# A two-layer hybrid decoder step: the input projection computed in another order of column blocks, and the gating norm's gain and shift moved behind its product

## The chip, the cores and the metric

One Trainium2 chip, one core, one launch. The metric is device time in microseconds (us). In the text PE is the matrix engine, DVE the vector engine, ACT the scalar engine, POOL the GpSimd engine and SP the engine whose queue issues almost all DMAs.

## What is computed

The program runs two layers (DEPTH = 2) over 512 prompt tokens and 32 sample tokens (8 sequences of 4). Each layer mixes tokens in four parallel ways and then runs a feed-forward block. The mixing part of the reference, cut to what matters:

```python
h = rms_norm(x, p['g_mix_pre'])
z = h @ p['w_in']                                   # 1024 -> 2048, fp32
a, ga, u, vb, q, k, v, xd = jnp.split(z, IN_SPLITS, axis=-1)   # 8 blocks of 256 columns
ya = silu(layer_norm(causal_depthwise_conv31(a * sigmoid(ga))))
# gating: LN(v) * g + b, then a causal 128x128 mix per head, plus bias, times gelu(u)
v = layer_norm(gelu(vb), p['sgu_ln_g'], p['sgu_ln_b'])
mixed = einsum('gts,bnsgc->bntgc', tril(w_s), v) + b_s
yb = gelu(u) * mixed
yc = rms_norm(diff_attend(q, k, v_att, lam), attn_sub_g)       # two softmax maps per head
yd = pool_mix(xd)                                   # windows 2, 4, 8, 16
x = x + rms_norm(concat([ya, yb, yc, yd]) @ p['w_out'], g_mix_post)
```

## The kernel before

Every fp32 weight is split into a high part (`whi`, a cast on ACT, line 190) and a low part (`wlo`, a subtraction on DVE, line 193), and a dense product takes three matmuls per 128 rows: high by high, high by low, low by high. The activations (`xhi`, `xlo`) are split in the same way.

`mixing` (one call per layer) walks over the eight 256-column blocks of `w_in` in the order of its table `order`, here by first column: 0 (`a`), 256 (`ga`), 1280 (keys), 1024 (queries), 1536 (values), 1792 (pooling), 512 and 768 (gating). Each block has two steps of 128 columns; each step has a first half (256 tokens) and, two steps later (`LAG = 2`), a second half (256 tokens and the 32 samples). Beside the steps run Python generators that emit the four mixers piece by piece: after each half step `advance` takes the next piece of every active one.

- `taps(c)` and `conv`: the gate product (line 410), then 30 chained multiply-adds of 512 columns on DVE per channel half (line 416), then LayerNorm and the swish. They can start when blocks 0 and 256 are complete.
- `stack`: keys and queries are split and copied by DMA into a 96-row layout. Per channel half that is one output DMA (line 468) and 24 small DMAs on the SP queue (line 478), which has the weight loads too.
- `attention`: per half 8 units of two score matmuls; DVE adds the bias `pb` and takes the minimum (line 501), ACT does the exponential (line 503), DVE forms the weighted difference (lines 511 to 513), PE transposes it (line 516), ACT copies it (line 518), PE multiplies with the values (`oT`).
- `gating`: per 128-token chunk a LayerNorm (lines 339, 340, 595), then a product with the gain and a sum with the shift (lines 596, 597), the causal mix on PE, the bias (line 607), the product (line 610) and a split.
- `pooling`: shifted sums on DVE (line 632).

The output projection (`project_last`, line 1259 onward) needs the split results `ya`, `yb`, `yc`, `yd` of all four. It runs eight turns of 24 matmuls; the first two use the first half of the output columns. In the order of the program the pieces are only a priority: a scheduler puts each engine's instructions in one fixed sequence when the program is built, and each engine then runs its own strictly in that sequence, waiting where one is not ready. The raw blocks of `w_in` have two buffers, the tiles named `t512` (key and query parts, gate) four, the score banks `s` two.

Of the kernel before, what the change touches and what calls it, by code (L numbers as in the profile page):

```python
# [8 lines left out]
F32 = mybir.dt.float32  # L9
# [111 lines left out]
def trunk(ctx, tc, A, O):  # L121
# [154 lines left out]
    def params(l, tp, bank):  # L276
        lam_init = 0.8 - 0.6 * math.exp(-0.3 * l)
        rows = tp.tile([72, 128], F32, tag="prow", name="prow")
        for i, n in enumerate(("conv_b", "conv_ln_g", "conv_ln_b", "pool_scale")):
            SY.dma_start(rows[2 * i:2 * i + 2, :], A[n][l].rearrange("(c p) -> c p", p=128))  # L280
        SY.dma_start(rows[8:70, :], A["conv_w"][l].rearrange("t (c p) -> (t c) p", p=128))
        for i in range(2):
            SY.dma_start(rows[70:71, 64 * i:64 * i + 64], A["attn_sub_g"][l:l + 1, :])
        o = psx(bank)
        T.transpose(o[:, :71], rows[:71, :], ident[:71, :71])
        pf, lm = PF[l][0], PL[l]
        V.tensor_copy(pf[:, :71], o[:, :71])
        V.tensor_scalar(pf[:, 72:76], pf[:, 2:6], 0.5, None, op0=ALU.mult)
        V.tensor_scalar(pf[:, 76:77], pf[:, 70:71], 1.0 - lam_init, None, op0=ALU.mult)
        lq = tp.tile([128, 4, 32], F32, tag="lq", name="lq")  # L290
        for i, n in enumerate(("lambda_q1", "lambda_q2", "lambda_k1", "lambda_k2")):
            SY.dma_start(lq[:, i, :], A[n][l, :].partition_broadcast(128))
        V.tensor_tensor(lq[:, 0:2, :], lq[:, 0:2, :], lq[:, 2:4, :], op=ALU.mult)
        V.tensor_reduce(lm[:, 0:2], lq[:, 0:2, :], axis=AX, op=ALU.add)
        S.activation(lm[:, 0:2], lm[:, 0:2], AF.Exp)
        V.tensor_tensor(lm[:, 2:3], lm[:, 1:2], lm[:, 0:1], op=ALU.subtract)
        V.tensor_scalar(lm[:, 3:4], lm[:, 2:3], -lam_init, None, op0=ALU.add)
# [50 lines left out]
    def mixing(l, mp, early):  # L348
# [32 lines left out]
        def ev_tmp(d, c, f, tag):  # L381
# [13 lines left out]
        order = [  # L395
            (0, [(0, ev_copy(hext[0], 0, 0.5, 30)), (1, ev_copy(hext[1], 1, 0.5, 30))]),
            (256, [(2, ev_ga(0)), (3, ev_ga(1))]),
            (1280, [(10, ev_tmp(kT, 0, 10, "kT")), (11, ev_tmp(kT, 1, 11, "kT"))]),
            (1024, [(8, ev_tmp(qT, 0, 8, "qT")), (9, ev_tmp(qT, 1, 9, "qT"))]),
            (1536, "v"),  # L400
            (1792, [(14, ev_copy(dext[0], 14, 1.0, 15)), (15, ev_copy(dext[1], 15, 1.0, 15))]),
            (512, [(4, ev_copy(uv[:, 0], 4)), (5, ev_copy(uv[:, 1], 5))]),
            (768, [(6, ev_copy(uv[:, 2], 6)), (7, ev_copy(uv[:, 3], 7))]),
        ]

# [52 lines left out]

        def stack():
            for c in range(2):  # L460
                st = ST[c] = {}
# [20 lines left out]
        def attention():  # L482
# [3 lines left out]
            for c in range(2):  # L486
# [20 lines left out]
                def weights(i, hh):  # L507
                    W = 128 * (i + 1)
                    P = Pm.pop((i, hh))
                    dn = den[:, i, hh]  # L510
                    V.reciprocal(dn[:, 2:3], dn[:, 1:2])
                    V.tensor_scalar(dn[:, 3:4], dn[:, 0:1], dn[:, 2:3], nlam, op0=ALU.mult, op1=ALU.mult)
                    V.scalar_tensor_tensor(P[0][:, :W], P[1][:, :W], dn[:, 3:4], P[0][:, :W], op0=ALU.mult, op1=ALU.add)
# [50 lines left out]
        def gating():  # L564
# [3 lines left out]
            for h in range(4):  # L568
                SY.dma_start(bsg[64 * (h % 2):64 * (h % 2) + 64, h // 2, :], A["sgu_b"][l, h, :].partition_broadcast(64))
            gr = mp.tile([128, 2, 256], F32, tag="sgr", name="sgr")  # L570
            SY.dma_start(gr[:, 0, :], A["sgu_ln_g"][l, :].partition_broadcast(128))
            SY.dma_start(gr[:, 1, :], A["sgu_ln_b"][l, :].partition_broadcast(128))
            o = acc()
# [8 lines left out]
            V.tensor_copy(bc, bsg[:, :, 0:4])  # L582
            SG[l] = (wc, bc)
            yield
            for f in (2, 0):
# [4 lines left out]
            for t in range(4):  # L590
# [4 lines left out]
                V.tensor_scalar(vn[:, t, :], o[:, :256], mean, r, op0=ALU.subtract, op1=ALU.mult)  # L595
                V.tensor_tensor(vn[:, t, :], vn[:, t, :], gr[:, 0, :], op=ALU.mult)
                V.tensor_tensor(vn[:, t, :], vn[:, t, :], gr[:, 1, :], op=ALU.add)
                yield
            y = yp.tile([128, 2, 2, SEQ], F32R, tag="y", name="yb")
            for c in range(2):  # L600
                o = acc()
                for n in range(4):
                    for hh in range(2):
                        h = 2 * c + hh
                        mm(o[64 * hh:64 * hh + 64, 128 * n:128 * n + 128], vn[:, n, 64 * h:64 * h + 64], wt[:, h, :])
                t = uv[:, 2 + c, :].rearrange("p (n t) -> p n t", n=4)
                V.tensor_tensor(t, o.rearrange("p (n t) -> p n t", n=4),
                                bsg[:, c:c + 1, :].to_broadcast([128, 4, 128]), op=ALU.add)
                tf = uv[:, 2 + c, :]
# [74 lines left out]
        def load(c0):  # L684
# [4 lines left out]
            else:  # L689
                pairs[c0] = raw_cols(w, c0, V, early.get(c0), None, G if c0 == 0 and early else None)  # L690

# [20 lines left out]
        for u in range(n + LAG):  # L712
# [17 lines left out]
            if b >= 0:  # L730
# [12 lines left out]
                if c0 == 256 and i == 1:  # L743
                    convs.append(taps(1))
                if c0 == 1024 and i == 1:
                    active.append(stack())
                if i == "v":
# [636 lines left out]
    with tc.tile_pool(name="pro", bufs=1, reuse_waits="tile") as pro, \  # L1384
# [6 lines left out]
        g = grow(pro, "g_mix_pre", 0)  # L1391
        early = {0: raw_load(A["w_in"][0], 0)}
        for t in range(2, 5):
            SY.dma_start(xs[t][:rows_of(t)], x_at(0)(128 * t, rows_of(t)))
        early[256] = raw_load(A["w_in"][0], 256)
        for t in range(5):
# [64 lines left out]
```

## Time and profile before

| | |
|---|---|
| median of 3 runs | 1454.04 us (1452.48 to 1457.04) |
| the profiled execution | 1448.71 us |
| its span, first to last instruction | 1446.8 us |
| PE busy / DVE / ACT / POOL | 1372.0 / 823.8 / 504.7 / 262.7 us |
| mean granted clock of PE | 0.978 of full |

The rest of the profiled execution (1.9 us) lies around the span. A busy share is an average over stages; the two mixing stages are about 14 to 192 us and 736 to 907 us of the span, and the feed-forward stages fill most of what is left.

### The profile page before, as it was taken

The numbers are of one execution on the slowest core, as the hardware profiler recorded it, in microseconds if no ns is written. First come the engines' busy times: TensorE is split into PE (matmuls) and PEld (weight loads), VectorE is DVE, ScalarE is ACT, GpSimd is POOL, SyncE is SP. The second block draws the span as 40 slices with busy tenths as digits, with TensorE's granted clock in tenths as the row PEclk, the third lists the DMA queues.
The fourth block names the chain that finished last, engine by engine and source line by source line (L and its number), as shares of the span: only waits on it lengthen the run. The fifth ranks groups of instructions, "written<-read, shape, count | busy, mean of one in ns | idle before, by whom it ended". The sixth has DMA issues, their size and how long they took to land.

```text
span 1446.8 us, 22864 instructions
## 1 busy us (share of the span) xinstructions
PE 1372.0 (95%) x9114; PEld 1078.7 (75%) x9114; DVE 823.8 (57%) x1660; ACT 504.7 (35%) x985; POOL 262.7 (18%) x271
## 2 busy tenths in 40 slices
PE   6999787999999999999989988989999999999997
PEld 6987576877666777777689976777776677768775
DVE  4986759866434333333669976778663333333344
ACT  4346634322224321222343474543322332222231
POOL 1000145455300000000220011544442000000003
PEclk9999799999999999999999997999999999999999
DMA  6452134888848752132434521468877496213132
GB/s 206 116 156 73 59 121 145 301 307 297 296 164 254 241 171 77 59 117 106 150 120 119 146 68 58 163 237 281 318 276 266 153 315 220 81 61 114 59 135 91
DMA packets 160091, 242.15 MB, mean 167 GB/s; under 512 B 10444, under 2 KB 118226, under 8 KB 159986
## 3 DMA queue, kind: packets, MB, share of 16 engines
q1 hardware_dynamic: 141410, 173.32, 37.1%
q0 software_dynamic: 18432, 67.12, 12.4%
q8 instruction: 72, 1.18, 0.3%
q14 instruction: 33, 0.27, 0.1%
q10 hardware_dynamic: 144, 0.26, 0.0%
HBM read 222.33 MB, written 12.04 MB: 162 GB/s over the span
## 4 chain that ended last, share of the span: by engine, by line
PE 81%; DVE 11%; ACT 2%; DMA 2%; issue 2%; POOL 1%; SPq 1%; DVEq 0%; POOLq 0%; ACTq 0%
PE acc L126 61%; PE sx L126 12%; PE ps L126 3%; DVE sca L872 2%; PE s L126 1%; DVE cacc L416 1%; DVE p L501 1%; DVE wlo L193 1%; DVE m L1301 1%; PE oT L126 1%; DVE x_t L1294 1%; ACT whi L190 1%; PE ps L516 1%; SPq L478 1%; PE ps L1001 1%
## 5 line engine op out<-in xcount | busy, mean ns | idle before, releaser
L126 PE MATMUL acc<-xhi,whi 128*128 128x512 f32 (+2 forms) x1152 | 405.5, 353 | 3.2 <-ACT whi L190 2.0
L126 PE MATMUL acc<-xhi,wlo 128*128 128x512 f32 (+2 forms) x1152 | 403.4, 351 | 0.2 <-DVE wlo L193 0.2
L126 PE MATMUL acc<-xlo,whi 128*128 128x512 f32 (+2 forms) x1152 | 402.0, 349 | 1.3 <-DVE xlo L238 1.3
L190 ACT CAST whi<-raw 128x1024 fp32r<-128x1024 f32 x178 | 184.3, 1048 | 333.7 <-PE acc L126 292.8
L193 DVE TENSOR_TENSOR wlo<-raw,whi 128x1024 fp32r<-128x1024 f32 x172 | 217.1, 1268 | 128.7 <-ACT whi L190 126.8
L126 PEld LDWEIGHTS acc<-xhi,whi 128*128 128x128 f32 x1152 | 217.1, 189 | 42.2 <-issue 8.0
L126 PEld LDWEIGHTS acc<-xlo,whi 128*128 128x128 f32 x1152 | 217.2, 189 | 31.9 <-issue 4.1
L126 PEld LDWEIGHTS acc<-xhi,wlo 128*128 128x128 f32 x1152 | 216.9, 188 | 31.5 <-issue 4.7
L126 PE MATMUL acc<-whi,h 128*128 128x512 f32 x704 | 226.7, 397 | 0.0
L126 PEld LDWEIGHTS acc<-whi,h 128*128 128x128 f32 x704 | 131.2, 188 | 44.1 <-issue 11.1
L126 PE MATMUL acc<-wlo,h 128*128 128x512 f32 x352 | 138.6, 395 | 0.0
L1276 POOL TENSOR_TENSOR m<-m,g_g_ffn_post 128x512 f32<-128x512 f32 x14 | 20.1, 1437 | 504.9 <-ACT junk L1275 504.9
L989 DVE STREAM_TRANSPOSE kt<-kr 128x1024 f32<-128x1024 f32 x64 | 78.5, 1233 | 27.6 <-DMA kr<-in_cache_k_dram,ik 23.3
L986 POOL DMA_INDIRECT kr<-in_cache_k_dram,ik x64 | 73.8, 1154 | 100.1 <-DVE kt L989 72.2
L416 DVE SCALAR_TENSOR_TENSOR cacc<-hext,pf,cacc 128x512 f32<-128x512 f32 x120 | 85.4, 747 | 0.6
L1345 DVE SCALAR_TENSOR_TENSOR th<-th,acc 128x512 f32<-128x512 f32 (+1 forms) x46 | 29.9, 649 | 87.2 <-PE acc L126 87.0
L126 PEld LDWEIGHTS acc<-wlo,h 128*128 128x128 f32 x352 | 66.1, 188 | 17.6 <-issue 4.5
L174 POOL TENSOR_TENSOR rsw<-rsw,mhalf 128x1 f32<-128x1 f32 (+2 forms) x62 | 39.1, 636 | 202.9 <-DVE rsw L173 189.4
L1016 POOL DMA_INDIRECT vr<-in_cache_v_dram,iv x64 | 63.2, 988 | 57.0 <-PE sx L126 41.2
L1154 DVE SCALAR_TENSOR_TENSOR sth<-sth,ps 128x64 f32<-128x64 f32 x22 | 4.8, 220 | 86.5 <-ACT sth L1153 86.5
L550 POOL TENSOR_TENSOR rse<-e,mhalf 128x8 f32<-128x8 f32 x4 | 8.5, 2130 | 242.7 <-DVE e L548 242.7
L126 PE MATMUL sx<-vr,pt 128*32 128x256 f32 x512 | 49.3, 381 | 0.0
(401 smaller groups left out, 1864.8 us busy)
## 6 DMA issues: line engine op xcount, KB each, us to landing
raw<-in_w_gu_dram SPq DMA_DIRECT2D x44, 1024.0 KB
raw<-in_w_down_dram SPq DMA_DIRECT2D x20, 1024.0 KB
rws<-in_w_gu_dram SPq DMA_DIRECT2D x40, 512.0 KB
raw<-in_w_in_dram SPq DMA_DIRECT2D x16, 1024.0 KB
raw<-in_w_out_dram SPq DMA_DIRECT2D x8, 1024.0 KB
rwo<-in_w_out_dram SPq DMA_DIRECT2D x16, 512.0 KB
rws<-in_w_down_dram SPq DMA_DIRECT2D x16, 512.0 KB
x<-x_t SPq DMA_DIRECT2D x12, 512.0 KB
```

The source lines that it names most:

```text
L126: T.matmul(out, lhsT, rhs, start=start, stop=stop)
L174: G.tensor_tensor(y, v, mhalf[:P, :n], op=ALU.pow)
L190: S.copy(hi, src)
L193: eng.tensor_tensor(lo, src, hi.bitcast(F32), op=ALU.subtract)
L416: V.scalar_tensor_tensor(a, hext[c][:, t:t + SEQ], pf[:, 8 + 2 * t + c:9 + 2 * t + c], a, op0=ALU.mult, op1=ALU.add)
L478: SY.dma_start(s[32 * g:32 * g + 32, jj, :].bitcast(F32), (hi, lo)[seqs[g]][32 * jj:32 * jj + 32, :].bitcast(F32))
L872: V.scalar_tensor_tensor(a[:, c], ext[:, c, :, t:t + 4], pf[:, 8 + 2 * t + c:9 + 2 * t + c], a[:, c], op0=ALU.mult, op1=ALU.add)
L986: G.indirect_dma_start(out=kr, out_offset=None, in_=ck, in_offset=bass.IndirectOffsetOnAxis(ap=ik[:, s, bg:bg + 1], axis=0))
L989: V.transpose(kt, kr)
L1016: G.indirect_dma_start(out=v.rearrange("p t e -> p (t e)"), out_offset=None, in_=cv, in_offset=bass.IndirectOffsetOnAxis(ap=iv[:, s, a:a + ...
L1276: (V if (t, half) == (3, 1) else G).tensor_tensor(m[t][:, hs], m[t][:, hs], gain[:, hs], op=ALU.mult)
L1345: V.scalar_tensor_tensor(th[:, :n], th[:, :n], 0.5, ou[:, :n], op0=ALU.mult, op1=ALU.mult)
```

## The change

The table `order` becomes keys, queries, values, `a`, `ga`, `u`, `vb`, pooling. `stack` takes the channel half as an argument and starts for each half as soon as its queries are complete. In gating, the gain is applied behind the causal mix (a per-partition factor, read from a parameter tile), and the shift goes through the same mix once per layer and is added to the bias. In attention the two reciprocals of a pair of heads become one instruction on two columns, and so do the two factors. The weights loaded ahead of the first layer are now blocks 1280 and 1024.

```diff
@@ params
+        SY.dma_start(rows[71:73, :], A["sgu_ln_g"][l].rearrange("(c p) -> c p", p=128))
-        T.transpose(o[:, :71], rows[:71, :], ident[:71, :71])
+        T.transpose(o[:, :73], rows[:73, :], ident[:73, :73])
+        V.tensor_copy(pf[:, 77:79], o[:, 71:73])
@@ mixing: order
-            (0, [(0, ev_copy(hext[0], 0, 0.5, 30)), (1, ev_copy(hext[1], 1, 0.5, 30))]),
-            (256, [(2, ev_ga(0)), (3, ev_ga(1))]),
             (1280, [(10, ev_tmp(kT, 0, 10, "kT")), (11, ev_tmp(kT, 1, 11, "kT"))]),
             (1024, [(8, ev_tmp(qT, 0, 8, "qT")), (9, ev_tmp(qT, 1, 9, "qT"))]),
             (1536, "v"),
-            (1792, [(14, ev_copy(dext[0], 14, 1.0, 15)), (15, ev_copy(dext[1], 15, 1.0, 15))]),
+            (0, [(0, ev_copy(hext[0], 0, 0.5, 30)), (1, ev_copy(hext[1], 1, 0.5, 30))]),
+            (256, [(2, ev_ga(0)), (3, ev_ga(1))]),
             (512, [(4, ev_copy(uv[:, 0], 4)), (5, ev_copy(uv[:, 1], 5))]),
             (768, [(6, ev_copy(uv[:, 2], 6)), (7, ev_copy(uv[:, 3], 7))]),
+            (1792, [(14, ev_copy(dext[0], 14, 1.0, 15)), (15, ev_copy(dext[1], 15, 1.0, 15))]),
@@ attention: weights
-                    V.reciprocal(dn[:, 2:3], dn[:, 1:2])
-                    V.tensor_scalar(dn[:, 3:4], dn[:, 0:1], dn[:, 2:3], nlam, op0=ALU.mult, op1=ALU.mult)
+                    if hh == 0:
+                        d2 = den[:, i]
+                        V.reciprocal(d2[:, :, 2:3], d2[:, :, 1:2])
+                        V.scalar_tensor_tensor(d2[:, :, 3:4], d2[:, :, 0:1], nlam, d2[:, :, 2:3], op0=ALU.mult, op1=ALU.mult)
@@ gating
-            gr = mp.tile([128, 2, 256], F32, tag="sgr", name="sgr")
-            SY.dma_start(gr[:, 0, :], A["sgu_ln_g"][l, :].partition_broadcast(128))
-            SY.dma_start(gr[:, 1, :], A["sgu_ln_b"][l, :].partition_broadcast(128))
+            gr = mp.tile([128, 256], F32, tag="sgr", name="sgr")
+            SY.dma_start(gr, A["sgu_ln_b"][l, :].partition_broadcast(128))
+            o = acc()
+            for h in range(4):
+                mm(o[64 * (h % 2):64 * (h % 2) + 64, 128 * (h // 2):128 * (h // 2) + 128], gr[:, 64 * h:64 * h + 64], wt[:, h, :])
+            V.tensor_tensor(bsg, o[:, :256].rearrange("p (c t) -> p c t", c=2), bsg, op=ALU.add)
-                V.tensor_tensor(vn[:, t, :], vn[:, t, :], gr[:, 0, :], op=ALU.mult)
-                V.tensor_tensor(vn[:, t, :], vn[:, t, :], gr[:, 1, :], op=ALU.add)
-                V.tensor_tensor(t, o.rearrange("p (n t) -> p n t", n=4),
-                                bsg[:, c:c + 1, :].to_broadcast([128, 4, 128]), op=ALU.add)
+                V.scalar_tensor_tensor(t, o.rearrange("p (n t) -> p n t", n=4), pf[:, 77 + c:78 + c],
+                                       bsg[:, c:c + 1, :].to_broadcast([128, 4, 128]), op0=ALU.mult, op1=ALU.add)
@@ the steps
-        def stack():
-            for c in range(2):
+        def stack(cs):
+            for c in cs:
-                if c0 == 1024 and i == 1:
-                    active.append(stack())
+                if c0 == 1024:
+                    active.append(stack([i]))
```

The table moves instructions in ways that the diff does not tell. Three places follow, first the SP queue of layer 0. Before, the bias `pb` and the weight blocks go out ahead of or among the small `st_k` and `st_q` DMAs:

```order
L571 DMA sgr<-in_sgu_ln_g_dram 128x256
L572 DMA sgr<-in_sgu_ln_b_dram 128x256
L484 DMA pb<-in_c_pbias_dram 128x512
L687 DMA raw<-in_w_in_dram 128x8x256
L198 DMA raw<-in_w_in_dram 128x8x256
L468 DMA out_dram<-ktok 128x4x128
...
L478 DMA st_k<-qkh 32x512
L198 DMA raw<-in_w_in_dram 128x8x256
L478 DMA st_q<-qkh 32x512 x5
```

In the changed program the same queue has all 48 small DMAs of both halves (the "..." holds 45 of them, and the second `ktok`) first, then the values' two output DMAs and the bias, and only then the four raw blocks 256, 512, 768 and 1792:

```order
L575 DMA sgr<-in_sgu_ln_b_dram 128x256
L470 DMA out_dram<-ktok 128x4x128
L480 DMA st_k<-qkh 32x512
L480 DMA st_k<-qkl 32x512
...
L480 DMA st_q<-qkl 32x512
L741 DMA out_dram<-vtok 128x4x256
L742 DMA out_dram<-vs 32x256
L486 DMA pb<-in_c_pbias_dram 128x512
L198 DMA raw<-in_w_in_dram 128x8x256 x4
```

So the bias and block 256 (`ga`) moved behind 48 small DMAs. In layer 1 of the changed program they did not; there the same queue reads:

```order
L486 DMA pb<-in_c_pbias_dram 128x512
L470 DMA out_dram<-ktok 128x4x128
L198 DMA raw<-in_w_in_dram 128x8x256
L480 DMA st_k<-qkh 32x512
L480 DMA st_k<-qkl 32x512
```

There the bias and block 256 stand ahead of the small DMAs, and the last three blocks behind them. The third place is DVE in layer 0. Before, the first gate product and the first taps (`cacc`) stand right behind the parameters:

```order
L193 TENSOR_TENSOR wlo<-raw,whi 128x1024
L410 SCALAR_TENSOR_TENSOR hext_231<-tg,hext_231 128x512
L296 TENSOR_TENSOR lam_81<-lam_81 128x1
L582 COPY bc_1814<-bsg 128x8
L413 TENSOR_SCALAR cacc_442<-hext_231,pf_82 128x512
L297 TENSOR_SCALAR lam_81<-lam_81 128x1
L416 SCALAR_TENSOR_TENSOR cacc_442<-hext_231,pf_82,cacc_442 128x512 x4
```

In the changed program they stand behind the attention of the first channel half, whose last weighted difference (line 517) is the second row here:

```order
L516 SCALAR_TENSOR_TENSOR den<-den,lam_81 128x2
L517 SCALAR_TENSOR_TENSOR p<-p,den 128x512 x2
L193 TENSOR_TENSOR wlo<-raw,whi 128x1024
L412 SCALAR_TENSOR_TENSOR hext_231<-tg,hext_231 128x512
L415 TENSOR_SCALAR cacc_1149<-hext_231,pf_82 128x512
L418 SCALAR_TENSOR_TENSOR cacc_1149<-hext_231,pf_82,cacc_1149 128x512 x6
L503 ISA p,mn<-s,pb 128x128
```

All 60 taps moved behind eight of the sixteen attention units; the other eight, and then gating, pooling and the norm of the convolution, stand among and behind the taps.

## Rows read from the trace of the kernel before

**Rows 1.** The page's busy time, share of the span and instructions by engine.

```profile
PE 1372.0 (95%) x9114; PEld 1078.7 (75%) x9114; DVE 823.8 (57%) x1660; ACT 504.7 (35%) x985; POOL 262.7 (18%) x271
```

**Rows 2.** Windows: us of stretch, then busy time of each engine, PE clock, DMA.

```profile
145.00:175.35 30.35, 19.53 (x126) 13.59 (x124) 23.72 (x79) 21.41 (x42) 6.91 (x9) 0.66 0.20 68
862.00:890.50 28.50, 21.03 (x125) 14.26 (x123) 22.96 (x78) 19.30 (x41) 5.09 (x9) 0.64 0.21 74
```

**Rows 3.** Timeline of PE: start, us, instruction, idle time before and its releaser.

```profile
144.71 0.29 PE L126 MATMUL acc<-xhi,wlo 128*128 128x288 f32 x1
...
175.35 0.50 PE L126 MATMUL acc<-whi,yd 128*128 128x512 f32 x1
...
188.50 0.50 PE L126 MATMUL acc<-whi,yc 128*128 128x512 f32 x1 [1.49 <-ACT yc L345]
...
192.29 0.50 PE L126 MATMUL acc<-whi,yd 128*128 128x512 f32 x1 [2.13 <-ACT whi L190]
...
907.40 0.61 PE L126 MATMUL acc<-whi,yd 128*128 128x512 f32 x1 [2.15 <-ACT whi L190]
```

**Rows 4.** DVE groups by line, in 25 to 255 us: busy us, mean ns, idle before.

```profile
L512 DVE TENSOR_SCALAR den<-den,lam 128x1 f32<-128x1 f32 x16 | 4.0, 266 | 0.1
...
L511 DVE RECIPROCAL den<-den 128x1 f32<-128x1 f32 x16 | 2.4, 157 | 5.9 <-ACT p L503 5.9
...
L597 DVE TENSOR_TENSOR vn<-vn,sgr 128x256 f32<-128x256 f32 x4 | 1.7, 417 | 0.1
L596 DVE TENSOR_TENSOR vn<-vn,sgr 128x256 f32<-128x256 f32 x4 | 1.6, 421 | 0.0
```

**Rows 5.** Timeline of DVE, layer 0 and the first row of layer 1.

```profile
40.42 0.68 DVE L410 SCALAR_TENSOR_TENSOR hext<-tg,hext 128x512 f32<-128x512 f32 x1
...
59.03 2.73 DVE L416 SCALAR_TENSOR_TENSOR cacc<-hext,pf,cacc 128x512 f32<-128x512 f32 x4
61.68 0.69 DVE L474 TENSOR_TENSOR qkl<-kT,qkh 128x512 fp32r<-128x512 f32 x1
...
94.34 0.42 DVE L501 CUSTOM_DVE_ANT_0 p<-s,pb 128x256 f32<-128x256 f32 x1
94.68 0.08 DVE L501 DVE_READ_ACCUMULATOR2_ANT mn<- 128x1 f32 x1
...
109.71 1.22 DVE L193 TENSOR_TENSOR wlo<-raw,whi 128x1024 fp32r<-128x1024 f32 x1
110.85 0.27 DVE L512 TENSOR_SCALAR den<-den,lam 128x1 f32<-128x1 f32 x1
...
188.48 0.69 DVE L346 TENSOR_TENSOR yc<-os__1975,yc 128x512 fp32r<-128x512 f32 x1 [0.68 <-ACT yc L345]
...
759.62 0.68 DVE L410 SCALAR_TENSOR_TENSOR hext<-tg,hext 128x512 f32<-128x512 f32 x1
...
903.59 0.69 DVE L346 TENSOR_TENSOR yc<-os__8388,yc 128x512 fp32r<-128x512 f32 x1 [0.68 <-ACT yc L345]
```

**Rows 6.** Windows: the DVE work of layer 0 from its second gate product.

```profile
52.89:188.20 135.31, 117.91 (x833) 103.80 (x831) 105.31 (x257) 70.98 (x161) 11.76 (x13) 0.91 0.33 97
```

**Rows 7.** Timeline of the SP queue: start and duration of each DMA issue, layer 0.

```profile
34.78 0.43 SPq L572 DMA_DIRECT2D sgr<-in_sgu_ln_b_dram  x1
35.25 0.43 SPq L484 DMA_DIRECT2D pb<-in_c_pbias_dram  x1
...
66.29 1.22 SPq L478 DMA_DIRECT2D st_k<-qkh  x2
67.55 0.59 SPq L478 DMA_DIRECT2D st_k<-qkl  x1
```

**Rows 8.** The chain of waits in 60 to 90 us: start, us, what.

```profile
68.88 5.22 DMA raw<-in_w_in_dram
...
79.11 2.03 DMA st_q<-qkl
```

**Rows 9.** Timeline of PE at the point up to which both programs run the same PE order.

```profile
38.18 0.27 PE L126 MATMUL acc<-xhi,whi 128*128 128x256 f32 x1
```

**Rows 10.** Windows: a stretch of dense projection alone.

```profile
25.00:50.00 25.00, 25.00 (x201) 24.66 (x201) 14.21 (x28) 7.93 (x20) 0.00 (x0) 1.00 0.39 115
```

More of the change, by code (lines that the diff above doesn't have):

```diff
@@ L277, in params @@
         lam_init = 0.8 - 0.6 * math.exp(-0.3 * l)
-        rows = tp.tile([72, 128], F32, tag="prow", name="prow")
+        rows = tp.tile([74, 128], F32, tag="prow", name="prow")
         for i, n in enumerate(("conv_b", "conv_ln_g", "conv_ln_b", "pool_scale")):
@@ L689, in load @@
             else:
-                pairs[c0] = raw_cols(w, c0, V, early.get(c0), None, G if c0 == 0 and early else None)
+                pairs[c0] = raw_cols(w, c0, V, early.get(c0), None, G if c0 == 1280 and early else None)
         def do_v(t, P, dst):
@@ L1391, in trunk @@
         g = grow(pro, "g_mix_pre", 0)
-        early = {0: raw_load(A["w_in"][0], 0)}
+        early = {1280: raw_load(A["w_in"][0], 1280)}
         for t in range(2, 5):
             SY.dma_start(xs[t][:rows_of(t)], x_at(0)(128 * t, rows_of(t)))
-        early[256] = raw_load(A["w_in"][0], 256)
+        early[1024] = raw_load(A["w_in"][0], 1024)
         for t in range(5):
```

## The prediction

> **What bounds the kernel now.** I read the page's busy times first. PE is busy for 1372.0 of 1446.8 us, DVE for 823.8 [rows 1], so over the whole span only PE can be the bound, and time can be won only where PE has gaps. The windows then show where these lie: behind the last projection matmul of each layer. In layer 0 that one starts at 144.71 us and the output projection at 175.35 [rows 3]. In this tail PE is busy for 19.53 of 30.35 us at a mean granted clock of 0.66, which is time at the 1.2 GHz level; layer 1 has 21.03 of 28.50 at 0.64 [rows 2]. DVE, with 23.72 and 22.96 us, is the busiest engine there. The reader is to see that the tail is attention, conv norm and gating handing small pieces from PE to DVE to ACT and back. The output projection then stops twice more: 1.49 us for `yc` and 2.13 us for a weight cast that stands behind `yc` on ACT [rows 3]. The change aims at these tails. So the question is what DVE does if attention moves forward, since attention, taps, pooling and gating all need it.
>
> **The parts with one answer.** In gating, 8 DVE operations per layer go (lines 596 and 597, mean 421 and 417 ns [rows 4]; they overlap, and by the 0.34 us that a 256-column operation takes start to start [rows 5] that is 2.8 us). Of the 16 reciprocals and 16 factors, 157 and 266 ns each, half go: 3.4 us by these durations, about 2.2 by the overlap. Four small matmuls, one 256-column sum and a parameter copy come in, under 1 us in all. One broadcast DMA goes and one two-row DMA comes. All this is on DVE or hidden, and it is in the sum below.
>
> **The SP queue in layer 0.** Up to 38.18 us PE runs the same order [rows 9]. There the change has its key transposes; with the copy to SBUF the first `ktok` DMA goes out at about 39.7. One small DMA holds the queue for 0.59 us, 0.63 start to start [rows 7]. 24 of them take 15.2 us, to 55.6. The second set of 24 waits until the first set's last sources are free, one landing later: the row has 2.03 us for such a DMA [rows 8]. So it runs from about 58.3 to 73.5. Then come two value DMAs, the bias at about 74.7 and block 256 at 75.3; before, the bias went out at 35.25 [rows 7]. The bias lands near 77.2 (the same 2.03 and a little for its size). A weight block takes 5.22 us [rows 8], so `ga` lands near 80.5 and, behind score exponentials and two casts on ACT, its first matmul can run near 82.7.
>
> PE meanwhile has 216 dense matmuls that need neither. At 25.00 / 201 = 0.124 us each [rows 10] they last 26.8 us, and PE stands at about 66.6 for a score bank that DVE empties only once it has the bias. From 66.6 to 82.7 it does little: some 14 us lost, and what follows starts at the lower clock. 144 matmuls later (18.3 us at 0.127, about 2 for the lower clock, 3.5 for attention pieces among them) block 256's second half is done and the first gate product can start on DVE: near **106.5 us, where before it started at 40.42** [rows 5].
>
> In layer 1 bias and block 256 stand ahead of the small DMAs. There is no stop; counting the same way from the shared start I get the first gate product at about **808.5, before 759.62** [rows 5].
>
> **What DVE still has to do from there.** The order puts on DVE behind the first gate product 60 taps, 2 gate products and 2 first taps, the second half of attention, 7 weight splits, pooling, gating, and the conv norm. Start to start the rows give 0.66 us for a tap (2.65 for four), 0.34 for a 256-column minimum, 1.14 for a split [rows 5], and 0.61 for other 512-column operations by the same reading. So: taps and gate 41.9; attention half 14.9 (16 minima 6.5, 8 differences 3.7, factors 1.1, two end pieces 3.6); splits 8.0; pooling 7.9; gating 7.9; conv norm 6.3. Sum 86.9 us. The same intervals on the instructions that stand in the old order from the second gate product to the last `yc` split give 104.0; the window shows 105.31 [rows 6], so I trust the sum to a few us. In layer 1 a little of the first half is left too: 88.5.
>
> DVE runs its list in order, with waits. In the old tail it idled 6.6 of 30 us [rows 2], and the new one ends in the same kind of hand-offs (chunk norms, the tanh of the conv output), so I add 8. Layer 0's last split comes at 106.5 + 86.9 + 8 = 201.4. Before, DVE finished its last split (`yc`) at 189.1 [rows 5], so **12 us later**. From there on the new order has 36 matmuls of the first two turns behind `ya`, near 10 us, where the old one reached its third turn at 192.29 [rows 3], 3 us after `yc`; that makes 19 us. Since DVE also paces the finishing of these turns, I take 14. Layer 1: 808.5 + 88.5 + 8 = 905.0 against 904.2; its third turn near 915 against 907.40 [rows 3]; between 1 and 7.5 I take 4. The stop for `yc` and for the cast behind it is gone in these numbers; what is late next is the conv mixer's `ya`.
>
> **Sum.** +14 and +4 give +18 us. On the profiled execution, 1448.71 us, that is 1467; the median of the runs stands 5.3 us above that execution, so I predict 1454 + 18 = **1472 us**. The bounds: with hand-off waits of 4 us and only the DVE ends compared, layer 0 loses 8 and layer 1 gains 3, +5; with 14 us of waits and the later third turns, 25 and 13.5, +38.
>
> **Rivals** (A is the forecast). *No stop in layer 0* (B): PE finds its data in time, because the small DMAs hold the queue for less than I take. Then the first gate product comes at about 91, DVE ends at 91 + 86.9 + 8 = 185.9, 3 us earlier than before, layer 1 keeps its +4, and the total is near 1455. Against it stand 48 issues that the trace shows at 0.59 each. The Trainium skill, "DMA: Bandwidth & Descriptors", section "Issuing engines are not separate DMA queues", says that the time to initiate a DMA is usually small beside the DMA; by it this rival would be the forecast. The trace does not agree for 64 KB copies: 0.63 of issue against 2.03 to land, and in a row of 48 the issue is what counts.
>
> *The tails go and nothing replaces them* (C, faster). The mechanism is DVE: if the first tap comes before about 189.1 - 86.9 - 8 = 94 us in layer 0 and 808 in layer 1, the old ends are beaten. With PE free of the stop, attention not holding it in layer 1 (tap at 795), and 2 us of waits, DVE ends at 180 and 885.5, 9 and 18.5 us earlier: with that PE's wait goes too, about 1427. For it speaks that DVE has 30 us of idle time in the old mixing stretch [rows 6]. Against it: that idle time was in the middle, and the change moves more of it to the front, where DVE has nothing but splits. The Trainium skill, "Perfetto Trace Analysis", section "Optimization Strategy", says that where the contended engine changes between regimes, interleaving them may help; by that this rival should win. The rows show the two regimes already interleaved before, with DVE the common part.
>
> *Heavier* (D): the stop in layer 0 also pushes the later weight blocks, or the in-order hand-offs cost 14 us and more: +30 to +40, near 1488.
>
> **How the numbers follow.** A 0.54, B 0.14, C 0.13, D 0.19. 0.3% is 4.4 us, about what a measurement of this kernel can tell from no change. A and D and a small part of B are slower: 0.75. B's rest is the same: 0.12. C: 0.13. The range leaves out C (0.13) and the far end of D. It goes from 1456, which is 3 below A's lower bound of 1454 + 5 and at B's value, to 1490, 2 short of A's upper bound of 1454 + 38 and just above D's value.
>
> **What would show it.** In the new profile: PE idle or nearly so from about 67 to 82 us, released by DVE's minimum, which waited for the bias DMA; the first gate product near 106 and 808; DVE busy 95% or more from there to about 165; the last split `ya`, not `yc`, the thing that PE's output projection waits for, near 201 and 905; no wait for `yc`. The prediction is wrong if the first gate product of layer 0 stands before 94, if DVE has more than 15 us of idle time behind it, or if the output projection begins before `ya` is on its way and does not stop for it.

## The result: slower by 3.4%, outside the range

The changed kernel takes 1504.67 us (median of 4 runs, 1501.95 to 1505.13) against 1455.24 for the kernel before; the ratio is 1.0337 (95% interval 1.0315 to 1.0360), which is 49 us. The forecast was 1472, the range 1456 to 1490. The direction was right, the size was not.

The page of the changed kernel, the line that answers to [rows 1]:

```profile
PE 1393.2 (93%) x9130; PEld 1092.4 (73%) x9130; DVE 819.7 (55%) x1616; ACT 501.0 (33%) x983; POOL 264.7 (18%) x271
```

DVE did 4 us less work in all, and the span grew from 1446.8 to 1503.4 us. (This is 56.6 us and not 49, since the profiled execution of before, 1448.71 us, was shorter than all four timed runs of that kernel.) PE was busy for 21 us more with nearly the same matmuls (9130 against 9114), at a mean granted clock of 0.960 instead of 0.978; the last section comes back to this. The other 35 us are idle time of PE: work waits. The SP queue in layer 0 follows, then DVE from the first piece that needs the bias (first column the start, second the duration; "..." marks rows left out):

```profile
74.28 0.91 SPq L486 DMA_DIRECT2D pb<-in_c_pbias_dram  x1
75.25 25.79 SPq L198 DMA_DIRECT2D raw<-in_w_in_dram  x4
```

```profile
77.93 0.29 DVE L503 CUSTOM_DVE_ANT_0 p<-s,pb 128x128 f32<-128x128 f32 x1 [17.94 <-DMA pb<-in_c_pbias_dram]
...
108.98 0.69 DVE L412 SCALAR_TENSOR_TENSOR hext<-tg,hext 128x512 f32<-128x512 f32 x1
...
180.51 0.43 DVE L341 BATCH_NORM_STATS2 bn<-acc 128x6 f32<-128x256 f32 x1 [3.14 <-PE acc L600]
...
211.23 0.69 DVE L348 TENSOR_TENSOR yd<-wn,yd 128x512 fp32r<-128x512 f32 x1 [2.85 <-ACT yd L347]
...
213.21 1.29 DVE L348 TENSOR_TENSOR ya<-cacc,ya 128x512 fp32r<-128x512 f32 x2
...
844.58 0.68 DVE L412 SCALAR_TENSOR_TENSOR hext<-tg,hext 128x512 f32<-128x512 f32 x1
...
952.27 1.29 DVE L348 TENSOR_TENSOR ya<-cacc,ya 128x512 fp32r<-128x512 f32 x2
```

Up to 108.98 us this is the picture of the forecast: the bias goes out at 74.28 (74.7 was worked out), DVE stands 17.94 us for it, and the first gate product comes at 108.98 (106.5), where it was at 40.42 [rows 5]. What stands behind it is not. The last split of `ya` ends at 214.5, not 201.4. PE in the same layer, with the idle time before an instruction and its releaser in brackets, and the first matmul of the third turn in both layers (the last row for layer 1):

```profile
78.28 0.69 PE L126 MATMUL s<-st_k,st_q 96*128 96x128 f32 x2 [13.27 <-DVE mn L503]
...
153.42 1.54 PE L520 MATMUL ps<-cst,p 128*128 128x128 f32 x6 [5.17 <-DVE p L517]
...
164.27 1.87 PE L126 MATMUL ps<-cst,sq 128*128 128x2 f32 x8 [1.34 <-ACT sq L544]
169.61 2.05 PE L126 MATMUL ps<-cst,rb 128*128 128x128 f32 x8 [3.47 <-DVE rb L556]
...
172.09 1.06 PE L578 MATMUL acc<-cst,wn 128*128 128x128 f32 x4
...
175.10 1.12 PE L126 MATMUL acc<-wt,sgr 128*64 128x128 f32 x8 [1.74 <-POOL wt L581]
176.15 0.61 PE L126 MATMUL acc<-xhi,whi 128*128 128x288 f32 x1
...
180.09 0.38 PE L600 MATMUL acc<-cst,uv 128*128 128x128 f32 x2
...
186.75 0.29 PE L126 MATMUL acc<-xhi,wlo 128*128 128x288 f32 x1
...
211.25 0.80 PE L126 MATMUL acc<-whi,yd 128*128 128x512 f32 x1 [2.13 <-ACT yd L347]
...
223.58 0.40 PE L126 MATMUL acc<-whi,yd 128*128 128x512 f32 x1
...
961.07 0.40 PE L126 MATMUL acc<-whi,yd 128*128 128x512 f32 x1
```

The dense projection now ends at 186.75 us, before at 144.71 [rows 3]. Its last 48 matmuls start at 176.15, behind the end of attention (`sq`, `rb`) and behind the weight transposes of gating (line 578); gating's norms and pooling come later still. The third turn is 31.3 us later in layer 0 (223.58 against 192.29). In layer 1 it is 53.7 later (961.07 against 907.40, both [rows 3]), so that layer adds 22.4. The windows behind the first gate product, layer 0 and then layer 1 (columns as in [rows 2]: the length, the busy time of PE, of its weight loads, of DVE, ACT and POOL, then PE's clock):

```profile
109.00:148.30 39.30, 39.25 (x305) 36.68 (x303) 35.65 (x80) 23.31 (x57) 1.90 (x1) 1.00 0.16 55
148.30:176.15 27.85, 14.85 (x74) 11.66 (x74) 27.48 (x49) 10.49 (x20) 3.22 (x2) 0.55 0.15 48
176.15:214.50 38.35, 24.32 (x124) 17.32 (x123) 26.73 (x64) 11.52 (x21) 4.63 (x10) 0.77 0.25 75
844.58:890.00 45.42, 42.67 (x339) 39.98 (x337) 41.92 (x94) 27.55 (x67) 2.09 (x1) 1.00 0.17 56
890.00:914.00 24.00, 10.72 (x62) 8.60 (x64) 21.09 (x36) 7.15 (x14) 3.22 (x2) 0.64 0.18 56
914.00:954.00 40.00, 26.60 (x133) 18.25 (x133) 28.95 (x68) 12.09 (x22) 6.63 (x11) 0.79 0.26 86
```

There are three stretches in each layer. First PE is full. Then DVE is full (27.48 of 27.85) with taps, and PE is half idle although dense work is left. Then neither is full: 24.32 and 26.73 of 38.35, a chain of hand-offs. DVE's idle time behind the gate product is 105.5 - 89.9 = 15.6 us in layer 0 and 109.4 - 92.0 = 17.4 in layer 1 (the three rows of each layer added up), where I had taken 8.

### The profile page after: what moved, and what is told of

Read it like the earlier page. It is cut to its first block, busy times and chain, and to the rows that moved or that the text cites. A ratio compares the mean times of both kernels' runs of the same rounds, so it can differ in the third digit from the quotient of the medians.

```text
span 1503.4 us, 22872 instructions
## 1 busy us (share of the span) xinstructions
PE 1393.2 (93%) x9130; PEld 1092.4 (73%) x9130; DVE 819.7 (55%) x1616; ACT 501.0 (33%) x983; POOL 264.7 (18%) x271
## 4 chain that ended last, share of the span: by engine, by line
PE 79%; DVE 10%; DMA 3%; SPq 2%; ACT 2%; issue 2%; POOL 1%; another core or an unknown queue 0%; DVEq 0%; POOLq 0%; ACTq 0%
PE acc L126 61%; PE sx L126 11%; PE ps L126 3%; SPq L480 2%; DVE cacc L418 2%; PE s L126 1%; DVE sca L877 1%; DVE wlo L193 1%; DMA raw<-in_w_in_dram 1%; PE oT L126 1%; DVE m L1306 1%; PE ps L1006 1%; DVE x_t L1299 1%; ACT whi L190 0%; POOL rsw L174 0%
## 5 line engine op out<-in xcount | busy, mean ns | idle before, releaser
L126 PE MATMUL acc<-xlo,whi 128*128 128x512 f32 (+2 forms) x1152 | 407.4, 354 | 1.8 <-DVE xlo L238 1.4
L126 PEld LDWEIGHTS acc<-xhi,whi 128*128 128x128 f32 x1152 | 221.7, 193 | 45.6 <-issue 10.1
L126 PEld LDWEIGHTS acc<-xlo,whi 128*128 128x128 f32 x1152 | 221.8, 193 | 33.1 <-issue 4.8
L126 PEld LDWEIGHTS acc<-xhi,wlo 128*128 128x128 f32 x1152 | 221.2, 192 | 32.6 <-issue 7.0
L503 DVE CUSTOM_DVE_ANT_0 p<-s,pb 128x128 f32<-128x128 f32 (+3 forms) x64 | 29.6, 485 | 40.5 <-PE s L126 22.2
```

Source lines behind the costliest of these rows:

```text
L126: T.matmul(out, lhsT, rhs, start=start, stop=stop)
L503: V.tensor_tensor_reduce(p[:, :W], sp[:, :W], pb[:, SEQ - W:], SLOPES[h], 3.0e38, ALU.add, ALU.min, mn)
```

## The experiments

The runs were made in five batches on several chips, each beside runs of the kernel before on its own chip (medians 1448.7 to 1456.2 us). So runs are compared by their ratio to before, and not by their medians; the last column is the ratio less 1, times 1455.2 us, and "by ratio" in the text means differences of it. The third turns are from each run's one profile, to be held against 192.29 and 907.40 [rows 3]. e3 and e11 leave out a part of the convolution; they are there to show what its time is worth.

| run | median, us | ratio to before (interval) | third turn, layers 0 / 1, us | against before, us |
|---|---|---|---|---|
| the change | 1504.7 | 1.0337 (1.0315 to 1.0360) | 223.6 / 961.1 | +49 |
| e1 bias and `ga` first | 1488.5 | 1.0229 (1.0212 to 1.0246) | 209.5 / 945.8 | +33 |
| e2 gating and pairs alone | 1451.2 | 0.9970 (0.9954 to 0.9986) | 184.5 / 906.9 | -4 |
| e3 15 taps | 1497.8 | 1.0292 (1.0259 to 1.0325) | 224.4 / 955.7 | +42 |
| e4 taps first | 1457.0 | 1.0015 (0.9998 to 1.0032) | 192.3 / 912.8 | +2 |
| e5 pooling early | 1490.8 | 1.0261 (1.0230 to 1.0293) | 217.5 / 945.3 | +38 |
| e8 gating blocks early | 1537.1 | 1.0569 (1.0538 to 1.0600) | 237.3 / 999.1 | +83 |
| e9 old table, rest changed | 1450.2 | 0.9976 (0.9964 to 0.9989) | 185.3 / 905.2 | -3 |
| e10 gating prepared early | 1479.4 | 1.0173 (1.0144 to 1.0202) | 207.1 / 938.0 | +25 |
| e11 the same, 13 taps | 1459.5 | 1.0082 (1.0063 to 1.0102) | 200.8 / 918.1 | +12 |
| e12 e1 and e10 | 1466.3 | 1.0126 (1.0110 to 1.0143) | 200.4 / 927.4 | +18 |
| e13 old table, prepared early | 1445.7 | 0.9979 (0.9969 to 0.9990) | 185.3 / 900.5 | -3 |
| e14 own buffer alone | 1480.7 | 1.0228 (1.0200 to 1.0255) | 215.9 / 942.1 | +33 |
| e15 early place alone | 1472.3 | 1.0170 (1.0146 to 1.0195) | 208.3 / 930.5 | +25 |

**e1: the stop in layer 0.**

```diff
-            SY.dma_start(pb, A["c_pbias"])
+            with tc.high_priority(2000):
+                SY.dma_start(pb, A["c_pbias"])
...
+                if c0 == 256:
+                    with tc.high_priority(2000):
+                        r0 = raw_load(w, c0)
```

> The changed kernel, with the bias and the load of block 256 put ahead of the 48 small key and query copies on the SP queue of layer 0. Theory 1 (the stop of PE in layer 0 delays the first gate product, and everything behind it on DVE keeps its distance): the stop of about 13 us before 78 us goes, the first gate product of layer 0 comes at 92 to 95 us instead of 108.98, the last split of ya of layer 0 some 15 us earlier than 213.2 us, and the time is 1504.7 - 15 = about 1490 us; layer 1 keeps its length. Rival (the hand-offs behind the taps set the end, not the start of the taps): the first gate product comes earlier, but ya by under 5 us, and the time stays above 1499 us.

The load of block 256 now goes out at 40.24 us, right behind the key output. In the second row, the summary of one line's instructions (durations, then the start of the first and of the last), layer 0's gate product comes at 96.7:

```profile
40.24 1.70 SPq L198 DMA_DIRECT2D raw<-in_w_in_dram  x1
```

```profile
L412 DVE SCALAR_TENSOR_TENSOR hext<-tg,hext x4: 684/686/687, 96.7 to 839.6; 128x512 f32<-128x512 f32 x4
```

16 us came off, as theory 1 had it, though the gate product came 2 us later than expected and `ya` 12 us earlier, not 15. From the gate product to the end of `ya` layer 0 took 105.8 us, in the changed kernel 105.5: the stop moved the start of this stretch and left its length. It was worth about what the forecast took for it (14 us).

**e2: the gating and the pairs alone,** on the kernel before.

> The kernel before with the gating norm's affine part behind the product and the paired reciprocals alone; the order of the blocks, the stacking and the early loads are those of before. Theory 1 (these two parts only take DVE work away, 5 us per layer, a part of it in the tail): 2 to 6 us faster than before, 1449 to 1453 us. Rival (the product of the shift, its sum and the longer way to the mix take the place of what goes): no change within 2 us, or slower by up to 4 us.

4 us faster (2 to 7 by the interval), theory 1. These parts are a gain; the loss is all in the order.

**e3: half the taps.**

```diff
-            for t in range(1, CW):
+            for t in range(1, 16):
```

> The changed kernel with 15 instead of 29 chained taps per channel half (the other half of the convolution is left out). 28 taps per layer at 0.66 us, start to start, are 18.5 us of DVE. Theory 1 (DVE bounds the stretch from the first gate product to the end of the taps, and what follows keeps its length): about 18 us less per layer, 1465 to 1472 us. Rival (PE's fixed order and the hand-offs among attention, gating and pooling set the end): under 6 us less per layer, 1493 us or more.

The rival: 6.5 us by ratio (within some 6 us either way). The whole chain is 30 taps per channel half and not 29, so 15 of each half were left out, 60 in both layers, about 40 us of DVE at 0.66 us each. Layer 0's third turn did not move at all (224.4 against 223.6). The windows of this run, and the last splits in layer 0:

```profile
148.30:176.15 27.85, 18.87 (x109) 15.34 (x108) 13.57 (x33) 11.63 (x23) 3.34 (x4) 0.69 0.15 49
176.15:212.30 36.15, 19.00 (x92) 12.54 (x91) 23.95 (x53) 11.38 (x20) 4.05 (x8) 0.69 0.19 65
```

```profile
189.66 1.29 DVE L348 TENSOR_TENSOR ya<-cacc,ya 128x512 fp32r<-128x512 f32 x2
...
211.60 0.69 DVE L348 TENSOR_TENSOR yd<-wn,yd 128x512 fp32r<-128x512 f32 x1 [3.60 <-ACT yd L347]
```

DVE fell from 27.48 to 13.57 us in the stretch where it had been full. `ya` ends at 191.0 instead of 214.5, but the last split of pooling, `yd`, ends at 212.3, as late as in the changed kernel (211.9), and the third turn stayed. So my theory fell in this form: DVE's amount of work does not set the end alone. A second chain, of attention, gating and pooling, runs beside the taps, and in layer 0 it ends within 3 us of them.

**e4: taps first** (0, 256, keys, queries, values, 512, 768, pooling).

> The changed kernel with blocks 0 and 256 first again, then keys, queries, values, 512, 768 and pooling last; the stacking by halves and the gating stay as changed. Theory 1 (the lost time comes from the taps starting late): the first gate product is back near 40 us and 760 us, the loss goes, 1445 to 1465 us. Rival (pooling last and attention within the rest make a longer chain behind the projection, whatever the taps do): still slower than before by 15 us or more, 1470 us or above.

Theory 1: the gate product is back at 38.1 us, and 47 of 49 us are gone. (This order also has the bias out at 34.13 us, so the stop of layer 0 goes with it, and the run does not tell the two apart.)

```profile
L412 DVE SCALAR_TENSOR_TENSOR hext<-tg,hext x4: 684/684/685, 38.1 to 771.2; 128x512 f32<-128x512 f32 x4
```

With the taps early, pooling last costs some 6 us by ratio (e4 against e9).

**e5 and e8: what stands in the tail.** e5 puts 1792 ahead of 512 and 768, e8 puts 512 and 768 ahead of 0 and 256.

> The changed kernel with block 1792 ahead of 512 and 768 (pooling within the projection, gating last, as before). Theory 2 (what ends a mixing stage is the chain of hand-offs behind the dense projection, that is the end of attention, gating, pooling, conv norm, in PE's fixed order; the taps are beside it): the pooling chain leaves the tail, 5 to 12 us less per layer, 1480 to 1495 us. Rival 1 (the amount of DVE work behind the first gate product sets the end): DVE has the same work there, 1500 to 1510 us.

> The changed kernel with the gating blocks 512 and 768 ahead of 0 and 256, so that gating runs within the projection and the taps start later still (about 18 us later per layer). Theory 2 (the chain of hand-offs behind the projection): the gating leaves the tail, the time falls although the taps start later, 1475 to 1497 us. Rival 1 (DVE's work behind the first gate product): the end comes later with the gate product, less the gating that goes ahead of it, some 10 us per layer: 1515 us or more.

They went opposite ways. e5 gained 11 us by ratio (14 by medians): theory 2, the tail's hand-offs count. e8 lost 34: theory 1, the taps count. Its gate product came not 18 but 50 us later (why so much was not followed up):

```profile
L412 DVE SCALAR_TENSOR_TENSOR hext<-tg,hext x4: 684/685/689, 159.0 to 927.8; 128x512 f32<-128x512 f32 x4
```

```profile
211.02 0.90 PE L441 MATMUL ps<-cst,cacc 128*128 128x128 f32 x3 [13.93 <-DVE cacc L418]
```

There the next matmul in PE's order is the convolution's, and it waits 13.93 us for the taps. Neither theory alone explains e3, e5 and e8 together. Two chains side by side do: whichever is longer ends the stage, and in layer 0 of the changed kernel they end at about the same time (211.9 and 214.5 us, above).

**e10, e14, e15: what holds gating back.** Gating's first tile, `wn`, is one of the four of `t512`, as are the closing tiles of attention (`os_`, `sq`, `rb`). e10 makes both edits below, e14 only the first, e15 only the second.

```diff
-            wn = mp.tile([128, 4, 128], F32, tag="t512", bufs=4, name="wn")
+            wn = mp.tile([128, 4, 128], F32, tag="sgw", name="wn")
...
+                if c0 == 256 and i == 1:
+                    gt = gating()
+                    next(gt)
                 if c0 == 768 and i == 1:
-                    active.append(gating())
+                    active.append(gt)
```

> The changed kernel with the gating's weight tile in a buffer of its own instead of one of the four of t512, and the gating's first piece (load, transposes, mask, product of the shift) emitted behind block 256; the order of the blocks is the changed one. PE's order then has the last dense matmuls among the attention of the second half and the gating's transposes ahead of the attention's end. Theory 2 (gating was locked behind the end of attention in PE's order): PE's idle time between 148 and 176 us shrinks to under half, the last split of the stage comes 10 us or more earlier in each layer, 1470 to 1486 us, with the first gate product unmoved near 109 us. Rival 1 (DVE's work behind the first gate product sets the end): no change, 1500 to 1510 us.

> The changed kernel with one edit: the gating's weight tile in a buffer of its own instead of one of the four of t512 that the end of attention uses too. In the built order the gating's weight transposes and its norm chunks then stand on PE ahead of the attention's closing products, and the last 48 dense matmuls among them. Theory 4 (the shared buffer is what put gating and the last dense work behind attention): it gives most of the 25 us of the early preparation, 1480 to 1490 us. Rival (the early emission did it, the buffer alone is too late to matter): 1497 us or more.

> The changed kernel with the other half of that edit: the gating's first piece is emitted behind block 256, and its weight tile keeps its place among the four buffers of t512. Theory 4: emitted early, the tile takes its turn in t512 ahead of the attention's closing tiles, so the lock goes in this way too, 1478 to 1488 us, as with both edits. Rival (the buffer is what counts): 1497 us or more.

e10 gives 24 us by ratio, e15 the same, e14 16. So the lock was real, and either edit opens it: the buffer alone for two thirds, the earlier place in the program for all. The clean case is e14, which has the same start and nearly the same DVE work behind it. Its windows from the gate product to the end of `ya`, layer 0 and layer 1, and two rows of PE in layer 0:

```profile
109.13:208.85 99.72, 74.72 (x505) 63.67 (x504) 88.70 (x190) 47.76 (x99) 10.71 (x13) 0.85 0.21 68
831.44:932.99 101.55, 76.93 (x532) 65.05 (x531) 90.31 (x194) 46.28 (x100) 12.23 (x13) 0.87 0.20 70
```

```profile
145.27 0.60 PE L578 MATMUL acc<-cst,wn 128*128 128x128 f32 x4
...
183.42 2.08 PE L126 MATMUL ps<-cst,rb 128*128 128x128 f32 x8
```

Gating's weight transposes now stand 38 us ahead of attention's closing product, where they stood behind it (172.09 and 169.61 above). DVE's idle time fell from 15.6 to 11.0 us in layer 0 and from 17.4 to 11.2 in layer 1. The windows of e10, layer 0 in three rows from its gate product to its last `ya` split, and layer 1 in one:

```profile
107.10:148.30 41.20, 39.40 (x316) 36.29 (x314) 38.24 (x69) 21.60 (x47) 1.34 (x1) 1.00 0.15 52
148.30:176.15 27.85, 13.21 (x80) 11.99 (x80) 27.63 (x55) 3.82 (x9) 5.36 (x5) 0.75 0.11 38
176.15:198.00 21.85, 14.41 (x54) 8.56 (x55) 17.21 (x39) 8.50 (x15) 3.65 (x7) 0.67 0.44 131
829.03:929.25 100.22, 77.42 (x529) 65.73 (x528) 90.01 (x194) 44.95 (x99) 12.36 (x13) 0.86 0.19 64
```

```profile
148.53 0.44 PE L600 MATMUL acc<-cst,uv 128*128 128x128 f32 x2 [1.25 <-ACT uv L593]
...
166.81 0.58 PE L126 MATMUL acc<-xhi,whi 128*128 128x288 f32 x1 [9.38 <-DVE vn L602]
```

Gating's first norm chunk is on PE at 148.53 instead of 180.09, and DVE does pooling and norms among the taps. The stretch in layer 0 is 90.9 us, 83.1 of DVE work and 7.8 idle. The taps start where they did (107.1), but 6.8 us of DVE work went out of the stretch: ten of the sixteen minima of attention's second half and what belongs to them now stand ahead of the gate product. So half of what e10 gains in layer 0 is this and half is idle time. In layer 1 the work stayed, 90.0 us, and the idle time is 10.2. One expectation failed: PE's idle time between 148 and 176 us did not shrink (14.6 against 13.0). PE now waits 9.38 us there for a norm on DVE that stands behind taps. What went away is the third stretch, 38.35 us before and 21.85 now.

**e11 and e12: what is left then.**

> The kernel with the gating's preparation early (1479.4 us) with 13 instead of 29 chained taps per channel half (the rest of the convolution is left out): 32 taps fewer per layer, 21 us of DVE at 0.66 us. In the changed kernel itself halving the taps gave 7 us over both layers. Theory 3 (two chains of about the same length run side by side behind the first gate product, the taps on DVE and the hand-offs of attention, gating and pooling on PE; each alone only frees the time down to the other): with the hand-offs already moved forward the taps now hold the end, and halving them gives over 16 us in both layers together, 1440 to 1463 us. Rival (the taps never held the end): under 8 us, 1471 us or more.

> The two moves together: the gating's preparation early (25 us by itself) and bias and block 256 ahead of the small copies on the SP queue of layer 0 (16 us by itself). Theory 3: they act on different stretches of layer 0 and add up nearly, 1504.7 - 25 - 16 = about 1464 us, still slower than before, because the taps start some 55 us later in layer 0 and some 50 in layer 1. Rival (both free the same time): 1474 us or more.

With gating freed, leaving out 17 taps of each half (about 45 us of DVE) gives 13 us by ratio, where leaving out 15 gave 6.5 in e3. (The two medians are 20 us apart, but the kernel before was 4 us faster on e11's chip.) That lies between the two expectations, and 13 and 6.5 are each uncertain by 5 to 6 us, so the totals alone don't show that the taps count for more now. The third turn of layer 0 points that way, in one profile of each: 6.3 us earlier than in e10, where e3's was 0.8 later than the changed kernel's. So e11 supports two chains without showing them. e12 was 7 us by ratio, not 16: at 1.0126 times 1455.2 it stands at 1473.6, which is the rival's 1474 and not theory 3's 1464. Its windows from the gate product at 90.1 us show why:

```profile
90.10:134.50 44.40, 43.07 (x349) 40.46 (x348) 40.77 (x93) 25.85 (x64) 3.58 (x2) 1.00 0.17 59
134.50:163.00 28.50, 18.33 (x114) 16.25 (x112) 26.89 (x54) 9.93 (x19) 4.29 (x4) 0.76 0.12 37
163.00:190.20 27.20, 16.40 (x67) 10.22 (x68) 23.07 (x50) 9.49 (x18) 4.38 (x7) 0.71 0.41 131
```

The gate product came 17 us earlier than in e10, and 90.7 us of DVE work stand behind it instead of 83.1: part of what DVE had done ahead of it now comes behind. The end moved by 8 us.

**e9 and e13: a version that beats both.** e9 has the old table with everything else changed, e13 adds the early preparation with its own buffer, emitted behind the values.

> The changed kernel with the whole table of before (0, 256, keys, queries, values, pooling, 512, 768); only the stacking by halves and the gating and reciprocals stay as changed. Against the run with the gating part alone this is the stacking by halves; against the run with taps first and pooling last it is the place of pooling. Theory 2: pooling last cost some 3 us per layer, so 1448 to 1453 us, as with the gating part alone. Rival (the stacking by halves costs or gives something by itself): more than 4 us away from 1451 us.

> The table of before with the gating and reciprocals as changed and the stacking by halves (1450.2 us), and the gating's preparation emitted early, behind the values, from a buffer of its own. Theory 3: the tail behind the projection of the old order has the gating's preparation in it as well, so 2 to 8 us less: 1442 to 1448 us, faster than both kernels. Rival (in the old order the gating waits for its own blocks, the last two of the table, and not for its weights): no change within 2 us of 1450 us.

Both stand with e2: 0.9970, 0.9976 and 0.9979, intervals all below 1. (The median of e13, 1445.7, would fit theory 3, but its chip ran the kernel before in 1448.7.) The stacking by halves gives nothing that shows, and preparing gating early gives nothing more in the old order (the rival): there gating waits for its own two blocks, which are last. So each of the three is faster than the kernel before by 3 to 4 us, and far faster than the changed one; none is shown to be better than the others.

## Why the forecast was wrong in size

- **What bounds the kernel** held: the time is lost in the mixing stages, where DVE and the hand-offs pace PE, and nearly all of it ahead of the third turns (53.7 of 56.6 us in the profiles).
- **The parts with one answer** (gating, pairs) held: a small gain, 4 us in e2.
- **The SP queue in layer 0** held. PE stopped for 13.27 us up to 78.28, the bias was out within half a microsecond of the time worked out, and e1 shows that the stop is worth 16 us. The Trainium skill, "DMA: Bandwidth & Descriptors", section "Issuing engines are not separate DMA queues", has the time to initiate a DMA as usually small beside the DMA; here one issue holds the queue for 0.63 us beside 2.03 to land [rows 7, rows 8], and the bias went out behind the whole row of 48, at 74.28.
- **Layer 1** had no stop, as forecast. Its gate product came at 844.58; less the 31.3 us by which layer 0's third turn came later that is 813.3, 5 us later than 808.5. Why is not known.
- **What DVE still has to do: the step that failed is "so I add 8".** 86.9 us of work was near (89.9 busy). But from gate product to the end of `ya` it took 105.5 and 109.0 us against 94.9 and 96.5. I had counted DVE's list and taken the hand-offs from the old tail, and had not followed PE's order to the end of the stage. There gating, pooling and 48 dense matmuls stood behind the closing products of attention. e14 shows it: with gating freed, the same start and nearly the same work (88.7 and 90.3 us), the idle time is 11.0 and 11.2 us, and the run is 16 us faster. The stretch misses the forecast by 10.6 us in layer 0 and 12.5 in layer 1. The 8 us of idle time, which were 15.6 and 17.4 (the forecast's upper bound took 14), are 7.6 and about 9 of it; the rest, some 3 us in each layer, is the sum of the work, which was too small. What the idle time still is above 8 with gating freed is not taken apart.
- **The cut** from 19 to 14 and from 7.5 to 4 us at the third turns had no row behind it, and was wrong: with DVE's end as measured, layer 0's third turn came 9 us behind `ya`, as worked out ("near 10"). That is 8.5 us.
- The sum of the misses: gate products 2.5 + 4.8, the stretch behind them 10.6 + 12.5, the cut 5 + 3.5, less 0.9 + 2.5 for third turns that came 9.1 and 7.5 us behind `ya` and not 10: 35.5 us. The third turns are 31.3 + 22.4 = 53.7 us late where 18 was forecast, which is 35.7 more.
- **The rivals.** D named the right mechanism ("the in-order hand-offs cost 14 us and more") and put it at 1488, still 17 us short; it deserved more than 0.19, since the rows could not bound a tail that did not exist yet, and the order of the changed program could. B's price for no stop, 1455, was wrong by as much as the forecast: e1 has no stop and takes 1488. C, that the tails go, is excluded by the result, and its rule for layer 0 (first tap before 94 us) was not enough either: e12 meets it (90.1) and is still 18 us slower than before. DVE then ends at 190.2, near the old 189.1, since 90.7 us of work and 9.4 idle stood behind the product; but the third turn comes 10 us behind `ya`, where it came 3 behind `yc`, at 200.4 against 192.29, and layer 1 loses another 12. The Trainium skill, "Perfetto Trace Analysis", section "Optimization Strategy", says that interleaving regimes with different contended engines may help. Here it cost 49 us: DVE was busy for most of both, 35.65 of 39.30 us beside the dense work and 27.48 of 27.85 with the taps.
- **What was to show it**: the first gate product, no wait for `yc`, and `ya` as the last split held; but in layer 0 PE stopped for `yd` (2.13 us at 211.25) and not for `ya`, pooling being as late as the rest. "DVE busy 95% or more to about 165" held from 148 on, not before (35.65 of 39.30). "More than 15 us of idle time behind it" was named as a sign of error, and came: 15.6.

Left open: how the remaining 18 us of e12 divide between the taps' late start and hand-offs. e4 and e9 show only that both go when the taps come first again.

## What to carry to other kernels

Where two engines hand work to each other in fixed orders, counting one engine's work behind an event is only a lower bound: follow the other engine's order through the same stretch as well, and look which unready piece stands ahead of ready work. Taking one of two chains of about equal length away shows little (half the taps, 40 us of DVE: 6.5 us), and that is not evidence that it was cheap. A tile of a shared rotating buffer orders its user behind everybody who takes a turn before it; a buffer of its own, or an earlier place in the program, was worth 16 and 24 us here.

## What the runs showed beyond the forecast

The waits also slowed the work between them. The eight matmuls on `rb`, which close the attention, took 2.05 us in the changed kernel (169.61 above), where the windows give a granted clock of 0.50 (first row; the 1.2 GHz level) after PE had been idle for 3.47 us just before. In e10 the same eight took 1.05 us, at 1.00 (second window, third row the instruction), straight behind 24 dense matmuls:

```profile
169.50:171.70 2.20, 2.09 (x10) 1.99 (x11) 2.13 (x3) 0.00 (x0) 0.00 (x0) 0.50 0.03 7
```

```profile
153.40:154.60 1.20, 1.20 (x13) 1.08 (x11) 1.14 (x3) 1.03 (x2) 0.89 (x1) 1.00 0.00 0
...
153.50 1.05 PE L126 MATMUL ps<-cst,rb 128*128 128x128 f32 x8
```

So here a chain of hand-offs pays twice, for the wait and then for the matmuls behind it. An estimate from these rows: the 14.85 us that PE was busy from 148.30 to 176.15 at a mean clock of 0.55 are about 8 at full clock. Whether the end would have come earlier by that was not tried, since the taps on DVE fill the same stretch. In e10 the mean clock of that stretch is 0.75 instead of 0.55.
